# Loading x transposed through ScalarE's queue instead of SyncE's, in a one-core decoder block

## The chip, the core and the metric

One Trainium2 chip, one of its cores. The metric is the device time of one execution in microseconds. Before the change three runs took 345.40, 346.83 and 347.18 us; the median is 346.83.

## What is computed

One layer of a decoder, 256 positions of width 1024, all in float32:

```python
hn = rmsnorm(x, g_attn)
qkv = hn @ w_in                               # 1024 x 3072
ya = rmsnorm(dilated_mixture(qa, ka, va), g_out_a)   # 8 heads
yb = rmsnorm(moba_attention(qb, kb, vb), g_out_b)    # 8 heads
h = x + concat(ya, yb) @ w_out
h = h + square(relu(rmsnorm(h, g_mlp) @ w_up)) @ w_down
gate = sigmoid(rmsnorm(h, g_ple) @ w_ple_gate + b_ple_gate)
h = h + gate * (p @ w_ple_proj)
return rmsnorm(h, g_final)
```

## The kernel before

Every float32 product is made of three matmuls (`mm3`, L149 to L153): each operand is split into a high part that TensorE takes in its fast float32 format and the rest, and high times high, high times low and low times high are summed. So each block of weights, once landed in a `raw` tile, is rounded by ScalarE into `hi` (L75) and the rest is taken by VectorE into `lo` (L76), and the activations are split likewise. The gain of a norm is multiplied into the weights by the same two instructions. The reciprocal root mean square of x is applied after the product: to the values by ScalarE (L419), to q and k by VectorE with a tile `rb` (L299, L300).

The first projection runs by k, the eight slices of 128 of the width: for each k the value weights (`slabs_in[0]`) against x, then the weights of two pairs of heads (`slabs_in[1]`). To let this start early, its loads are cut into small pieces that SyncE's queue issues in the order of use (L203 to L226): `head`, which holds the gains and x for k = 0, then for each k the two weight blocks, and between them `xT` for k = 1, for 2 and 3, and for 4 to 7 (`x_load`, L210). ScalarE's first instructions are a copy that makes it load its table of functions (L202), and then the splits of x and the weights as they land.

While k runs, ScalarE and VectorE sum the squares of x (`x_squares`, L256). At step 33 of the first unit `x_stats` (L274) sums them over the features with two small matmuls (L271), takes mean plus epsilon on VectorE (L183) and its power of -1/2 on GpSimd (L184), and makes a diagonal matrix of it on VectorE (L278). At step 42 `x_bcast` (L282) spreads it over the partitions with two matmuls (L285), and VectorE copies the result to `rb` (L286). At step 46 `make_bias` (L311) has GpSimd make the bias of the first pair of heads out of `consts`: two operations at L316 and two at L318. A bias has two buffers. Scores follow (`scores`, L320): twelve matmuls at L328, evacuated by VectorE with the bias (L334, L337), exponentials on ScalarE (L343), their scaling on GpSimd (L349), transposes on TensorE (`turn`, L359), and the product with the values (L371, L372).

The steps of the units are written in one order. A scheduler of the framework then orders each engine's instructions by its own estimate of when their inputs are there, under the constraint that `issue_after` (L133, L138) sets at the places shown. So an engine's order can move where the source does not. SyncE's and ScalarE's queues share eight semaphore lanes for their transfers: a transfer waits on its queue until the one that had its lane last has landed.

```python
{33: [x_stats], 42: [x_bcast], 46: [VE(0), B_(0, 0)], 48: [E_(0, 0)]}   # L480
```

Of the kernel before, what the change touches and what calls it, by code (L numbers as in the profile page):

```python
# [32 lines left out]
def block_kernel(ctx: ExitStack, tc: tile.TileContext, a: dict):  # L33
    nc = tc.nc
# [135 lines left out]
    stat = outer.tile([P, 64], F32, name="stat")  # L170
    mhalf = outer.tile([P, 2], F32, name="mhalf")
# [23 lines left out]
    xT = ap.tile([P, KT, S], F32, tag="xy", name="xT")  # L195
# [3 lines left out]
    for s in slabs_in[0] + slabs_in[1]:  # L199
        s.raw = wraw.tile([P, 4, 512], F32, tag="raw", name="raw")  # L200
        s.load = lambda: None
    nc.scalar.copy(stat[:, 63:], mhalf[:, :1])  # L202
    nc.sync.dma_start(head, a["head"])  # L203
    halves = [slice(0, 256), slice(256, 512)]

    def block_load(u, k0, k1, col=slice(0, 512)):
        s, r = slabs_in[u][k0 // 4], slice(k0 % 4, (k1 - 1) % 4 + 1)
        nc.sync.dma_start(s.raw[:, r, col], s.src[:, r, col])  # L208

    def x_load(k0, k1):  # L210
        nc.sync.dma_start(xT[:, k0:k1], a["xT"][:, k0:k1])

    for col in halves:
        block_load(0, 0, 1, col)
    block_load(1, 0, 1)
    x_load(1, 2)
    for u in range(2):
        block_load(u, 1, 2)
    x_load(2, 4)
    for k in (2, 3):  # L220
        for u in range(2):
            block_load(u, k, k + 1)
    x_load(4, 8)
    for k in (4, 6):
        for u in range(2):
            block_load(u, k, k + 2)  # L226
# [574 lines left out]
```

## Time and profile before

| What | Value |
|---|---|
| median of three runs | 346.83 us |
| the profiled execution | 347.6 us |
| its span, first to last instruction | 345.8 us |
| mean granted clock of TensorE | 0.982 |
| busy: TensorE, VectorE, ScalarE, GpSimd | 333.2, 216.8, 199.8, 74.1 us |
| DMA, mean over the span | 176 GB/s |

The profile is of one execution, 0.8 us above the median. Busy time alone does not tell where time can be had: the views that do are the waits of each engine, its instructions in order of time, and the chain of waits that ended last. Lines in the rows are those of the kernel before; behind the change all lines from L227 on are smaller by one.

### The profile page before, as it was taken

The numbers are of one execution on the slowest core, as the hardware profiler recorded it, in microseconds if no ns is written. First come the engines' busy times: TensorE is split into PE (matmuls) and PEld (weight loads), VectorE is DVE, ScalarE is ACT, GpSimd is POOL, SyncE is SP. The second block draws the span as 40 slices with busy tenths as digits, with TensorE's granted clock in tenths as the row PEclk, the third lists the DMA queues.
The fourth block names the chain that finished last, engine by engine and source line by source line (L and its number), as shares of the span: only waits on it lengthen the run. The fifth ranks groups of instructions, "written<-read, shape, count | busy, mean of one in ns | idle before, by whom it ended". The sixth has DMA issues, their size and how long they took to land.

```text
span 345.8 us, 5641 instructions
## 1 busy us (share of the span) xinstructions
PE 333.2 (96%) x2188; PEld 298.9 (86%) x2188; DVE 216.8 (63%) x380; ACT 199.8 (58%) x378; POOL 74.1 (21%) x103
## 2 busy tenths in 40 slices
PE   8899899999999999999999999999999999999990
PEld 8699779899877889898998988989989899888890
DVE  4789948687837769537537275292553843758563
ACT  6786838677664668728255374373652825458431
POOL 0025563455214001311020110110201102000443
PEclk9999969999999999999999999999999999999996
DMA  7998951404444369653727618357194463700011
GB/s 193 372 401 289 316 187 53 160 33 159 163 170 159 112 236 321 206 213 115 261 116 248 237 46 320 123 173 263 51 327 159 136 242 110 243 2 1 2 62 61
DMA packets 10971, 60.87 MB, mean 176 GB/s; under 512 B 1216, under 2 KB 1984, under 8 KB 4416
## 3 DMA queue, kind: packets, MB, share of 16 engines
q1 hardware_dynamic: 10944, 60.51, 49.4%
q8 instruction: 17, 0.28, 0.4%
q14 instruction: 10, 0.08, 0.1%
HBM read 59.46 MB, written 1.05 MB: 175 GB/s over the span
## 4 chain that ended last, share of the span: by engine, by line
PE 92%; DMA 2%; POOL 2%; DVE 1%; SPq 1%; ACT 0%; issue 0%; POOLq 0%; DVEq 0%
PE ps L151 29%; PE ps L152 28%; PE ps L153 28%; DMA raw<-in_w_in 2%; PE ps L328 2%; PE ps L371 2%; PE ps L359 2%; PE ps L519 1%; POOL pb L349 1%; SPq L208 1%; PE ps L372 1%; POOL bias L318 1%; DVE lo L76 0%; POOL bias L316 0%; PE ps L271 0%
## 5 line engine op out<-in xcount | busy, mean ns | idle before, releaser
L76 DVE SCALAR_TENSOR_TENSOR lo<-raw,head,hi 128x512 fp32r<-128x512 f32 (+2 forms) x137 | 105.0, 813 | 24.9 <-ACT hi L75 24.6
L75 ACT ACTIVATE hi<-raw,head 128x512 fp32r<-128x512 f32 (+2 forms) x137 | 92.7, 733 | 25.2 <-PE ps L152 11.1
L151 PE MATMUL ps<-hhi,hi 128*128 128x256 f32 x256 | 72.6, 283 | 0.0
L153 PE MATMUL ps<-hhi,lo 128*128 128x256 f32 x256 | 72.5, 283 | 0.0
L152 PE MATMUL ps<-hlo,hi 128*128 128x256 f32 x256 | 72.4, 283 | 0.0
L84 DVE TENSOR_TENSOR lo<-raw,hi 128x1024 fp32r<-128x1024 f32 x34 | 41.5, 1254 | 28.1 <-ACT hi L83 28.0
L583 POOL TENSOR_TENSOR sq<-r 128x512 f32<-128x512 f32 (+1 forms) x18 | 19.9, 1108 | 141.8 <-ACT r L581 141.8
L151 PE MATMUL ps<-hi,u 128*128 128x512 f32 x128 | 50.2, 392 | 0.0
L83 ACT ACTIVATE hi<-raw 128x1024 fp32r<-128x1024 f32 x34 | 34.3, 1052 | 27.2 <-PE ps L153 25.5
L152 PE MATMUL ps<-lo,u 128*128 128x512 f32 x128 | 49.9, 390 | 0.0
L153 PE MATMUL ps<-hi,u 128*128 128x512 f32 x128 | 49.8, 389 | 0.0
L152 PEld LDWEIGHTS ps<-hlo,hi 128*128 128x128 f32 x256 | 49.1, 192 | 0.3
L151 PEld LDWEIGHTS ps<-hhi,hi 128*128 128x128 f32 x256 | 49.1, 192 | 0.3
L153 PEld LDWEIGHTS ps<-hhi,lo 128*128 128x128 f32 x256 | 49.1, 192 | 0.0
L151 PE MATMUL ps<-xhi,hi 128*128 128x256 f32 x128 | 38.7, 303 | 0.0
L152 PE MATMUL ps<-xlo,hi 128*128 128x256 f32 x128 | 36.9, 289 | 0.0
L153 PE MATMUL ps<-xhi,lo 128*128 128x256 f32 x128 | 36.7, 289 | 0.0
L586 DVE TENSOR_TENSOR u<-sq,u 128x512 fp32r<-128x512 f32 (+1 forms) x18 | 11.7, 650 | 34.0 <-ACT u L585 34.0
L153 PEld LDWEIGHTS ps<-hi,u 128*128 128x128 f32 x128 | 24.0, 188 | 5.1
L151 PEld LDWEIGHTS ps<-hi,u 128*128 128x128 f32 x128 | 24.1, 188 | 4.7
L152 PEld LDWEIGHTS ps<-lo,u 128*128 128x128 f32 x128 | 24.1, 188 | 4.7
L151 PEld LDWEIGHTS ps<-xhi,hi 128*128 128x128 f32 x128 | 25.2, 197 | 1.5 <-issue 0.7
(128 smaller groups left out, 531.7 us busy)
## 6 DMA issues: line engine op xcount, KB each, us to landing
raw<-in_w_up SPq DMA_DIRECT2D x16, 1024.0 KB, 5.1
raw<-in_w_down SPq DMA_DIRECT2D x16, 1024.0 KB, 4.8
raw<-in_w_in SPq DMA_DIRECT2D x8, 1024.0 KB, 7.2
raw<-in_w_out SPq DMA_DIRECT2D x4, 1024.0 KB, 4.9
raw<-in_w_gate SPq DMA_DIRECT2D x4, 1024.0 KB, 5.1
raw<-in_w_in SPq DMA_DIRECT2D x4, 512.0 KB, 8.8
raw<-in_w_in SPq DMA_DIRECT2D x7, 256.0 KB, 7.0
h_sb<-in_x SPq DMA_DIRECT2D x1, 1024.0 KB, 7.4
```

Of the source, the lines that this page charges most:

```text
L75: nc.scalar.activation(h, r, AF.Copy, scale=sc)
L76: nc.vector.scalar_tensor_tensor(l, r, sc, h.bitcast(F32), op0=ALU.mult, op1=ALU.subtract)
L83: nc.scalar.activation(h, r, AF.Copy)
L84: nc.vector.tensor_tensor(l, r, h.bitcast(F32), op=ALU.subtract)
L151: nc.tensor.matmul(ps, lhs[0], rhs[0], start=start, stop=False)
L152: nc.tensor.matmul(ps, lhs[0], rhs[1], start=False, stop=False)
L153: last_mm[0] = nc.tensor.matmul(ps, lhs[1], rhs[0], start=False, stop=stop)
L328: last_mm[0] = nc.tensor.matmul(ps[h][:, c : c + w], d["q"][a_][r, q0 : q0 + P], d["k"][b_][r, :w], start=i == 0, stop=i == 2)
L359: nc.tensor.transpose(ps[:, c * P : (c + 1) * P], d["p"][:, h, c * P : (c + 1) * P], ident)
L371: nc.tensor.matmul(o[:, :S], v[:, 0, cols], d["pT"][h][:, :S], start=True, stop=False)
L583: nc.gpsimd.tensor_tensor(sq, r, r, op=ALU.mult)
L586: nc.vector.tensor_tensor(o[1], sq, o[0].bitcast(F32), op=ALU.subtract)
```

## The change

The three transfers of `xT` are issued by ScalarE's queue, ahead of the copy that loads its table. SyncE's queue keeps `head`, the weights and the tables.

```diff
-    nc.scalar.copy(stat[:, 63:], mhalf[:, :1])
     nc.sync.dma_start(head, a["head"])
...
     def x_load(k0, k1):
-        nc.sync.dma_start(xT[:, k0:k1], a["xT"][:, k0:k1])
+        nc.scalar.dma_start(xT[:, k0:k1], a["xT"][:, k0:k1])
+
+
+    x_load(1, 2)
+    x_load(2, 4)
+    x_load(4, 8)
+    nc.scalar.copy(stat[:, 63:], mhalf[:, :1])
     for col in halves:
         block_load(0, 0, 1, col)
     block_load(1, 0, 1)
-    x_load(1, 2)
-    for u in range(2):
-        block_load(u, 1, 2)
-    x_load(2, 4)
-    for k in (2, 3):
+    for k in (1, 2, 3):
         for u in range(2):
             block_load(u, k, k + 1)
-    x_load(4, 8)
     for k in (4, 6):
         for u in range(2):
             block_load(u, k, k + 2)
```

On ScalarE's queue, at the start of the program, the issues stand ahead of the table load (`stat` is the copy's target, `xhi` the high part of x). Before:

```order
L202 ACT_TABLE_LOAD
L202 COPY stat<-mhalf 128x1 [waits DVE_49]
L230 ACTIVATE xhi<-head 128x256 [waits DMAHW0_49]
L261 ACTIVATE xsq<-head 128x256
L75 ACTIVATE hi<-raw,head 128x256 [waits DMAHW1_49]
```

and now:

```order
L210 DMA xT<-in_xT 128x256
L210 DMA xT<-in_xT 128x512
L210 DMA xT<-in_xT 128x1024
L216 ACT_TABLE_LOAD
L216 COPY stat<-mhalf 128x1 [waits DVE_49]
L229 ACTIVATE xhi<-head 128x256 [waits DMAHW1_49]
L75 ACTIVATE hi<-raw,head 128x256 [waits DMAHW3_49]
```

Three issues have come in front, and the square of the first slice has gone behind the first splits of weights.

On GpSimd, behind the constants at the program's start, the scheduler gives another order too. Before, the power of x's mean square (`stat<-stat,mhalf`) is first, and two biases follow, (0, 0) and (0, 1):

```order
L184 ISA
L184 TENSOR_TENSOR stat<-stat,mhalf 128x2 [waits DVE_49]
L316 TENSOR_SCALAR bias<-consts 128x256 [waits DMAHW3_49]
L316 TENSOR_SCALAR bias<-consts 128x256
L318 TENSOR_TENSOR bias<-bias,consts 128x256 [waits Pool_49] x2
L316 TENSOR_SCALAR bias<-consts 128x256 x2
L318 TENSOR_TENSOR bias<-bias,consts 128x256 [waits Pool_49] x2
L316 TENSOR_SCALAR bias<-consts 128x256 [waits DVE_49]
```

and now:

```order
L315 ISA
L315 TENSOR_SCALAR bias<-consts 128x256 [waits DMAHW3_49]
L315 TENSOR_SCALAR bias<-consts 128x256
L317 TENSOR_TENSOR bias<-bias,consts 128x256 [waits Pool_49] x2
L315 TENSOR_SCALAR bias<-consts 128x256 x2
L317 TENSOR_TENSOR bias<-bias,consts 128x256 [waits Pool_49] x2
L184 TENSOR_TENSOR stat<-stat,mhalf 128x2 [waits DVE_49]
L315 TENSOR_SCALAR bias<-consts 128x256 [waits DVE_49]
```

The power has moved behind both biases and so behind the landing of `consts`.

On VectorE, from the mean square of x (L183) to the first evacuations of q and k, before:

```order
L183 TENSOR_SCALAR stat<-ps_339 128x2 [waits PE_49]
L278 TENSOR_SCALAR diag<-ident,stat 128x128 [waits DMAHW1_49,Pool_49]
L278 TENSOR_SCALAR diag<-ident,stat 128x128
L76 SCALAR_TENSOR_TENSOR lo<-raw,head,hi 128x512 [waits DMAHW2_49,Activation_49]
L76 SCALAR_TENSOR_TENSOR lo<-raw,head,hi 128x512 [waits Activation_49] x3
L286 COPY rb<-ps_384 128x256 [waits PE_49]
L299 TENSOR_TENSOR q<-ps_242,rb 128x256 [waits DVE_49,PE_49]
```

and now:

```order
L183 TENSOR_SCALAR stat<-ps_339 128x2 [waits PE_49]
L277 TENSOR_SCALAR diag<-ident,stat 128x128 [waits DMAHW1_49,Pool_49]
L277 TENSOR_SCALAR diag<-ident,stat 128x128
L76 SCALAR_TENSOR_TENSOR lo<-raw,head,hi 128x512 [waits DMAHW2_49,Activation_49]
L76 SCALAR_TENSOR_TENSOR lo<-raw,head,hi 128x512 [waits Activation_49] x3
L76 SCALAR_TENSOR_TENSOR lo<-raw,head,hi 128x512 [waits DMAHW4_49,Activation_49]
L76 SCALAR_TENSOR_TENSOR lo<-raw,head,hi 128x512 [waits Activation_49]
L285 COPY rb<-ps_384 128x256 [waits PE_49]
L76 SCALAR_TENSOR_TENSOR lo<-raw,head,hi 128x512
L298 TENSOR_TENSOR q<-ps_242,rb 128x256 [waits DVE_49,PE_49]
```

Two splits of the next weights have come between the diagonal and `rb`, and one more between `rb` and q. Further on, the four evacuations of the first scores (L334, L337; now L333, L336) stand in one piece, where two splits and a split of k stood among them.

## Rows read from the trace of the kernel before

**Rows 1.** The waits of TensorE (PE) over the whole execution: the waiting line, the one that ended the wait, us in total, how many, the longest in us.

```profile
PE ps L359 <- POOL pb L349: 2.3, 2, 2.0
PE ps L151 <- ACT hi L75: 1.1, 1, 1.1
...
PE ps L152 <- DVE lo L76: 0.3, 1, 0.3
```

**Rows 2.** Busy time by stage: the stretch and its length in us, then busy us and number of instructions of PE, PE's weight loads, VectorE, ScalarE and GpSimd, the granted clock of PE, the busy share of the DMA engines and what they moved in GB/s.

```profile
0.00:50.00 50.00, 45.35 (x312) 41.23 (x314) 38.02 (x83) 34.12 (x73) 17.27 (x29) 0.93 0.86 303
50.00:100.00 50.00, 50.00 (x395) 44.80 (x392) 36.55 (x106) 34.29 (x94) 20.81 (x36) 1.00 0.34 128
```

**Rows 3.** Two pieces of the chain of waits that ended last: start in us, length in us, what it was. The first is the transfer of the value weights for k = 2, the second six transposes of a later pair of heads at full clock.

```profile
4.48 6.98 DMA raw<-in_w_in
...
55.13 0.66 PE ps L359 x6
```

**Rows 4.** TensorE's instructions in order of time: start in us, length in us, engine, line, operation, what it writes from what, tile, how many, and in brackets the idle time in front of it and what ended it.

```profile
12.26 0.50 PE L151 MATMUL ps<-hi,xhi 128*128 128x512 f32 x1 [1.06 <-ACT hi L75]
13.05 0.50 PE L152 MATMUL ps<-lo,xhi 128*128 128x512 f32 x1 [0.28 <-DVE lo L76]
...
27.47 0.61 PE L285 MATMUL ps<-diag,ones 128*128 128x128 f32 x4
...
33.71 0.91 PE L328 MATMUL ps<-k,q 64*128 64x256 f32 x12
...
36.43 0.28 PE L151 MATMUL ps<-xhi,hi 128*128 128x256 f32 x1
...
38.59 0.28 PE L151 MATMUL ps<-xhi,hi 128*128 128x256 f32 x1
...
41.29 0.28 PE L153 MATMUL ps<-xhi,lo 128*128 128x256 f32 x1
43.58 0.90 PE L359 MATMUL ps<-ident,pb 128*128 128x128 f32 x3 [2.01 <-POOL pb L349]
44.81 0.90 PE L359 MATMUL ps<-ident,pb 128*128 128x128 f32 x3 [0.33 <-POOL pb L349]
45.36 0.56 PE L151 MATMUL ps<-xhi,hi 128*128 128x256 f32 x1
...
49.48 0.99 PE L371 MATMUL ps<-pT,vt 128*64 128x256 f32 x4
```

**Rows 5.** One microsecond behind those transposes, columns: length, busy us and instructions of PE, granted clock, DMA share, GB/s.

```profile
47.00:48.00 1.00, 1.00 (x6) 0.50 0.72 164
```

**Rows 6.** The three issues of xT by SyncE's queue: line, queue, operation, shortest, median and longest duration in ns, first and last start.

```profile
L211 SPq DMA_DIRECT2D xT<-in_xT x3: 432/442/1331, 2.6 to 6.4; - x3
```

**Rows 7.** DMA in two microseconds of the start, columns as in rows 5.

```profile
4.00:5.00 1.00, 1.00 (x7) 1.00 0.74 132
...
12.00:13.00 1.00, 0.50 (x1) 1.00 1.05 424
```

**Rows 8.** ScalarE's first instructions in order of time, columns as in rows 4.

```profile
0.72 1.28 ACT L202 ACT_TABLE_LOAD   x1 [0.72 <-PEq L794]
...
2.99 0.42 ACT L230 ACTIVATE xhi<-head 128x256 fp32r<-128x256 f32 x1 [0.79 <-DMA head<-in_head]
```

**Rows 9.** GpSimd's instructions in order of time, columns as in rows 4: the power, the biases of the first two head pairs, and the third bias with the scaling of the first probabilities.

```profile
23.91 0.72 POOL L184 TENSOR_TENSOR stat<-stat,mhalf 128x2 f32<-128x2 f32 x1 [23.49 <-DVE stat L183]
24.72 1.50 POOL L316 TENSOR_SCALAR bias<-consts 128x256 f32<-128x256 f32 x2
...
29.87 1.44 POOL L318 TENSOR_TENSOR bias<-bias,consts 128x256 f32<-128x256 f32 x2
38.70 1.21 POOL L316 TENSOR_SCALAR bias<-consts 128x256 f32<-128x256 f32 x2 [7.39 <-DVE nm L337]
...
41.87 2.89 POOL L349 TENSOR_SCALAR pb<-pb,nm 128x256 f32<-128x256 f32 x4
```

**Rows 10.** The transfer of consts by its line: durations of the issue in ns with first and last start, and us from issue to landing.

```profile
L240 SPq DMA_DIRECT2D consts<-in_consts x1: 432/432/432, 15.1 to 15.1; - x1
...
DMA to landing us min/median/max: 8.8/8.8/8.8
```

**Rows 11.** The two kinds of operation that make a bias, by line: shortest, median and longest duration in ns.

```profile
L316 POOL TENSOR_SCALAR bias<-consts x16: 403/406/931, 24.7 to 79.2; 128x256 f32<-128x256 f32 x16
...
L318 POOL TENSOR_TENSOR bias<-bias,consts x8: 731/738/1184, 26.3 to 47.4; 128x256 f32<-128x256 f32 x8
```

**Rows 12.** VectorE's instructions in order of time, columns as in rows 4: splits of weights (L76), the diagonal, q's and k's splits, the score evacuations of the second pair of heads from the first to the split behind the last.

```profile
17.49 1.41 DVE L76 SCALAR_TENSOR_TENSOR lo<-raw,head,hi 128x512 fp32r<-128x512 f32 x2
...
24.66 0.63 DVE L278 TENSOR_SCALAR diag<-ident,stat 128x128 f32<-128x128 f32 x2 [0.84 <-POOL stat L184]
25.21 3.84 DVE L76 SCALAR_TENSOR_TENSOR lo<-raw,head,hi 128x512 fp32r<-128x512 f32 x4
...
32.44 0.41 DVE L304 TENSOR_TENSOR q<-q 128x256 fp32r<-128x256 f32 x1
32.78 0.41 DVE L306 TENSOR_TENSOR k<-k 128x256 fp32r<-128x256 f32 x1
...
43.99 0.41 DVE L334 CUSTOM_DVE_ANT_0 sc<-ps,bias 128x256 f32<-128x256 f32 x1
...
45.10 0.74 DVE L76 SCALAR_TENSOR_TENSOR lo<-raw,head,hi 128x512 fp32r<-128x512 f32 x1
```

## The prediction

> **What bounds the kernel now.** I read the waits of TensorE first. Over the whole execution it has three that matter, 2.3, 1.1 and 0.3 us [rows 1]; the rows of TensorE below place them all ahead of 45 us. The busy table says the same by stage: TensorE has 45.35 us of work in the first 50 and is busy for all of the next 50 [rows 2]. So the end of the program is the moment at which TensorE comes out of the first 50 us, plus work that never waits; what the change does there goes to the end one for one, and what it does to any other engine counts only where TensorE then waits.
>
> Next the early part. TensorE's wait of 1.1 us ends when the block of value weights for k = 2 has landed and been split; the chain of waits shows this transfer taking 6.98 us from its issue at 4.48 [rows 3]. The last place is the transposes of the first pair of heads (L359): matmuls stop at 41.57 (41.29 plus 0.28), the transposes start at 43.58 and at 44.81, and the matmuls behind them run at 45.36 to 49.48 what the same 18 matmuls did from 36.43 to 38.59 [rows 4]: 4.12 us against 2.16, since the granted clock in that stretch is 0.50, the 1.2 GHz level [rows 5]. Six transposes at full clock take 0.66 us [rows 3], here 1.78. So this place costs 2.01 + 1.12 + 1.96 = 5.1 us.
>
> **The change, part by part.**
>
> SyncE's queue loses three issues, which took 0.43, 0.44 and 1.33 us of it [rows 6]: the weights behind each are issued up to 0.4, 0.9 and 2.2 us sooner. That is cover, not gain: the block that TensorE waited for was issued at 4.48 and spent 6.98 us after that [rows 3], so its bytes, not its issue, were late. I count one effect on the transfers. In the fifth microsecond the engines moved 132 GB/s, against 424 in the thirteenth [rows 7]; with a second queue holding work this dip should mostly close, some 0.2 MB or 0.5 us at the later rate. Bounds: nothing saved, or all 2.2 us of issue.
>
> The Trainium skill speaks against more than that: its page "DMA: Bandwidth & Descriptors", section "Issuing engines are not separate DMA queues", says that starting transfers from several engines saves only the sequencer's time to start them. By that rule the dip would stay too and the sum below would be 0.5 us longer.
>
> ScalarE gets the three issues ahead of its table load. Load and copy run from 0.72 to 2.20 (2.99 less the idle 0.79), and the first activation at 2.99 waits for the transfer of head [rows 8]. No row shows an issue on ScalarE; nearest are SyncE's 0.43 to 1.33 [rows 6]. At 0.44 each they take 1.3, so the first activation comes at 0.72 + 1.3 + 1.5 = 3.5, 0.5 late; the upper bound, 2.2 us in all, makes it 1.4 late. Both are covered by the next term; without that cover they would go to the end.
>
> GpSimd is where the change is largest, though the diff does not touch it. The power that makes x's reciprocal root mean square (L184) stood first and ran at 23.91; behind it came the eight operations that make the biases of two head pairs, to 31.31 [rows 9]. In the changed order the eight come first. They wait for consts, issued at 15.1 and landed 8.8 us later, at 23.9 [rows 10]; the same bytes stand in front of it as before, so I take 23.4 with the 0.5 from above (bounds 21.7 and 24.9, the later one if the transfer ahead of it is issued a microsecond late because its buffer is split later). The eight cost between 4 x 0.406 + 4 x 0.738 = 4.6 us by their medians [rows 11] and 6.6 us as they ran [rows 9]. I take 4.8, the medians and 0.2 for hand-overs, because the slow ones ran beside VectorE's splits of 25.21 to 29.05 [rows 12] and now VectorE will stand at the diagonal, waiting for this very power. That gives 28.2; the power adds 0.72 [rows 9] and a hand-over, 29.0; the diagonal 0.63 [rows 12], 29.7. TensorE's two broadcast matmuls (L285) need it and stand ahead of every later matmul. They ran at 27.47 [rows 4], when the diagonal had been ready since 25.29, a slack of 2.2. Now they run at 29.8: **+2.3 us** (0.4 to 5.6 by the bounds). What is hidden under it: a TensorE that reaches L285 up to 2.3 late.
>
> VectorE's order behind the diagonal changes as well. Six splits instead of four stand ahead of rb. A split takes 0.70, or 0.96 beside GpSimd, q's or k's split about 0.34 [rows 12]. From the diagonal, 6 x 0.70, rb 0.35, a split 0.70, three evacuations of 0.35, a split 0.70 and two of 0.34: 7.7 us until k's lower part is there. TensorE comes to the scores 6.24 us after L285 (33.71 less 27.47) [rows 4]. It can start two of the matmuls without that part: a wait of about **+1.2 us**.
>
> Then the transposes again. Behind k: split, evacuation, two small ones, two splits, 3.2 us, so 10.9 after the diagonal; the four score evacuations, now in one piece, took 1.11 from 43.99 to 45.10 [rows 12], 12.0. GpSimd then makes the third bias and scales: 38.70 to 41.87, and from there 1.71 to the first transpose and 2.94 to the second [rows 4, 9]: 16.9 and 18.1 after the diagonal. TensorE, from its scores at 7.5, needs 7.86 (33.71 to 41.57) [rows 4] and is there at 15.4. It waits 1.5 instead of 2.01. Whether the clock falls decides the rest. It fell after a wait of 2.01 with another 0.9 behind the first three transposes; it did not after 1.06 and 0.28 about 12 us [rows 4, 7]. Now 1.5 and 0.9 are due, 2.4 in all, nearer to the 2.9: I take it that it falls, for 1.5 + 1.12 + 1.96 = 4.6. If it stays, 2.6.
>
> The sum: 2.3 + 1.2 + 4.6 - 5.1 = **+3.0 us**. The profiled execution took 347.6 around its span of 345.8, 0.8 above the median of 346.83; on the median the forecast is 349.8.
>
> **The rivals.**
>
> Even: the same delay, but the clock stays at its upper level at the transposes. 2.3 + 1.2 + 2.6 - 5.1 = +1.0, 347.8. For it: the wait is shorter than the one that dropped the clock. If instead TensorE pays at L285 with a drop, it comes to the scores later, does not wait there, and the transposes find their data: the same end within half a microsecond.
>
> Faster: the transfers gain more than their order says, consts lands so early that the biases are done before the power's input is there, and the weights end TensorE's early waits. TensorE would reach L285 by 26.2 (27.47 less 1.06 and 0.28 [rows 4]), so the power must end by 25.4, the biases by 24.6 and consts land by 19.8, 4.1 us sooner than now. From there the gain is 1.3 plus some 1.5 of the wait at the transposes, 344.0. For it: several seconds of the early table are far below 424 GB/s [rows 7]. Against it: the same 6.5 MB stand in front of consts.
>
> Slower still: x's 896 KB share the engines with the first weights. The blocks for k = 1 and 2 then have up to 512 KB more in front, 1.2 us at 424 GB/s and 4.0 at 132 [rows 7], and ScalarE starts 0.5 to 1.4 late. Below 2.3 all of it is hidden under L285; above, TensorE itself is late. With 3.8 the sum is 1.5 longer: 351.3. For it: in the fifth microsecond the weights had the engines almost alone with 128 KB of x, and were slow already [rows 7].
>
> The Trainium skill, in the same page, section "Queues, rings and completion order", has each engine take turns between the queues that hold work, a packet at a time. By this x and the weights would share from the first packet, which is this rival's mechanism; no row here shows two loaded queues.
>
> **How the numbers follow.** A change within 0.5% (1.7 us) is about what a measurement of this kernel can't tell from none. Chances: forecast 0.40, even 0.30, faster 0.15, slower still 0.15. Of the forecast's 0.40 the bounds of consts and of the biases put about 0.05 within 0.5%; of slower still 0.03 comes out even, because later waits absorb it; of even 0.03 goes over the line. So slower 0.40 - 0.05 + 0.12 + 0.03 = 0.50, same 0.35, faster 0.15. The range runs from 345.0, which leaves out most of the faster case, to 352.3, which holds slower still and the forecast with biases at 6.6; about 2 in 10 is outside. The likeliest case alone spans 347.9 to 352.
>
> **What would show it.** Right: in the changed profile GpSimd's first work is a bias that starts at about 23.4 as consts lands, L184 ends near 29, VectorE idles behind L183 until its diagonal, and TensorE has a wait of 1 to 3 us ahead of L285 (L284 in the new numbering) that ends with the diagonal; then a short wait at the scores, and one of 1 to 2 us at the transposes with the clock at 0.50 behind it. Wrong: consts landed at 20 or before, or TensorE at L285 without a wait, or its longest wait ahead of the value weights of k = 1 or 2 with the clock low there. If the first activation comes later than 4.2, an issue on ScalarE costs more than SyncE's rows say.

## The result

The changed kernel takes 350.29 us (median of 4 runs, 349.11 to 350.89) against 346.53 for the kernel before (4 runs): ratio 1.010, 95% interval 1.007 to 1.013. It is slower, by 3.8 us.

The profiled execution took 349.11 around a span of 347.3, 1.5 more than that of before. Its mean granted clock is 0.995, and its clock did not fall behind the first transposes. The other three runs have no trace, only a mean of 0.977 to 0.982. In the traces of this study, a mean of 0.982 or 0.983 goes with a long stretch at a clock of 0.50 at the transposes (43.4 to 50.2 us in the kernel before; also experiments 3 and 7), 0.990 or 0.991 with a shorter one (47.7 to 51.1 in experiment 1; also 4 and 10, and 2 behind its broadcast), and 0.992 or more with none there (the changed kernel, 5, 6, 8, 9 and 11). The kernel before mixes likewise: of 82 runs beside the experiments, 9 with a mean of 0.994 or more have a median of 345.20, 54 with 0.987 to 0.991 have 346.3, and 19 with less have 347.64. Like with like, the change costs 349.11 - 345.20 = 3.9 us without a fall, by one run, and 350.65 - 347.64 = 3.0 with the long one, if those three fell like that.

**TensorE.** The first fence holds its waits over the whole execution (columns of [rows 1]).

```profile
PE ps L358 <- POOL pb L348: 2.8, 2, 1.7
PE ps L151 <- ACT hi L75: 2.4, 2, 1.4
...
PE ps L151 <- DVE rb L285: 0.6, 1, 0.6
```

The waits at the transposes remain, the two for weights have moved from 12 us to the very start, and there is none at the broadcast L284, where the prediction looked for one of 1 to 3 us. In order of time (columns of [rows 4]):

```profile
5.79 0.80 PE L151 MATMUL ps<-hi,xhi 128*128 128x256 f32 x2 [1.43 <-ACT hi L75]
...
8.48 0.58 PE L151 MATMUL ps<-hi,xhi 128*128 128x256 f32 x1 [0.95 <-ACT hi L75]
...
11.94 0.41 PE L153 MATMUL ps<-xhi,lo 128*128 128x256 f32 x1
12.15 0.41 PE L151 MATMUL ps<-xhi,hi 128*128 128x256 f32 x1
...
12.53 0.28 PE L153 MATMUL ps<-xhi,lo 128*128 128x256 f32 x1
12.64 0.40 PE L151 MATMUL ps<-hi,xhi 128*128 128x512 f32 x1
...
30.14 0.68 PE L284 MATMUL ps<-diag,ones 128*128 128x128 f32 x4
34.56 0.38 PE L151 MATMUL ps<-xhi,hi 128*128 128x256 f32 x1 [0.55 <-DVE rb L285]
...
37.26 1.07 PE L327 MATMUL ps<-k,q 64*128 64x256 f32 x12
...
47.00 0.55 PE L358 MATMUL ps<-ident,pb 128*128 128x128 f32 x3 [1.70 <-POOL pb L348]
48.66 0.55 PE L358 MATMUL ps<-ident,pb 128*128 128x128 f32 x3 [1.11 <-POOL pb L348]
```

The matmuls of k = 1 (the first 128x512 one) start at 12.64; before they started at 7.91. Until 12.4 matmuls of 256 columns follow each other every 0.21 us, from 12.53 every 0.12. Three rows of the kernel before tell what that means: the start of its k = 1, and two like matmuls in the microsecond of [rows 5], 0.22 apart at a granted clock of 0.50:

```profile
7.91 0.63 PE L151 MATMUL ps<-hi,xhi 128*128 128x512 f32 x2
...
47.00 0.41 PE L152 MATMUL ps<-xlo,hi 128*128 128x256 f32 x1
47.22 0.41 PE L153 MATMUL ps<-xhi,lo 128*128 128x256 f32 x1
```

So TensorE ran at the 1.2 GHz level until 12.4, with waits of 1.43 and 0.95 us in that time. At L284 it is 2.67 us later than in [rows 4]: 2.06 of the 4.73 are made up, 1.34 of them because the waits of [rows 4] at 12 and 13 us are gone.

**GpSimd and VectorE** (columns of [rows 9], [rows 12]):

```profile
24.12 0.90 POOL L315 TENSOR_SCALAR bias<-consts 128x256 f32<-128x256 f32 x2 [23.70 <-DMA consts<-in_consts]
...
28.95 0.72 POOL L184 TENSOR_TENSOR stat<-stat,mhalf 128x2 f32<-128x2 f32 x1
42.20 1.64 POOL L315 TENSOR_SCALAR bias<-consts 128x256 f32<-128x256 f32 x2 [12.53 <-DVE nm L336]
...
45.53 3.06 POOL L348 TENSOR_SCALAR pb<-pb,nm 128x256 f32<-128x256 f32 x4
```

```profile
29.71 0.48 DVE L277 TENSOR_SCALAR diag<-ident,stat 128x128 f32<-128x128 f32 x2 [3.35 <-POOL stat L184]
30.11 4.06 DVE L76 SCALAR_TENSOR_TENSOR lo<-raw,head,hi 128x512 fp32r<-128x512 f32 x6
34.09 0.42 DVE L285 COPY rb<-ps 128x256 f32<-128x256 f32 x1
```

The diagonal is being finished as TensorE arrives at L284: two delays end at the same moment, and no wait shows which one counts.

**Queues.** Two issues on SyncE, ScalarE's first instructions (columns of [rows 8]), and two microseconds of DMA (columns of [rows 7]):

```profile
15.77 0.33 SPq L60 DMA_DIRECT2D raw<-in_w_in  x1
16.14 0.43 SPq L239 DMA_DIRECT2D consts<-in_consts  x1
```

```profile
0.72 1.38 ACTq L210 DMA_DIRECT2D xT<-in_xT  x3
...
3.70 0.42 ACT L229 ACTIVATE xhi<-head 128x256 fp32r<-128x256 f32 x1
5.23 0.51 ACT L75 ACTIVATE hi<-raw,head 128x256 fp32r<-128x256 f32 x1 [1.11 <-DMA raw<-in_w_in]
7.92 0.51 ACT L75 ACTIVATE hi<-raw,head 128x256 fp32r<-128x256 f32 x1 [2.18 <-DMA raw<-in_w_in]
```

```profile
4.00:5.00 1.00, 0.36 (x4) 1.00 0.93 290
...
17.00:18.00 1.00, 1.00 (x11) 1.00 0.89 254
```

The fifth microsecond now moves 290 GB/s where [rows 7] have 132, but what it moves is x: ScalarE waits 1.11 and 2.18 us for the two halves of the first value weights. Consts is issued at 16.14, a microsecond later than in [rows 10]: the transfer ahead of it is issued at 15.77, since its buffer waits for a split that VectorE now starts at 14.99, and at 17 us the DMA engines are down to 254 GB/s. Before, that transfer was issued at 14.68:

```profile
14.68 0.33 SPq L60 DMA_DIRECT2D raw<-in_w_in  x1
```

### The profile page after: what moved, and what is told of

Read it like the earlier page. It is cut to its first block, busy times and chain, and to the rows that moved or that the text cites. A ratio compares the mean times of both kernels' runs of the same rounds, so it can differ in the third digit from the quotient of the medians.

```text
span 347.3 us, 5638 instructions
## 1 busy us (share of the span) xinstructions
PE 332.7 (96%) x2188; PEld 298.3 (86%) x2188; DVE 215.1 (62%) x380; ACT 200.0 (58%) x378; POOL 72.2 (21%) x103
## 4 chain that ended last, share of the span: by engine, by line
PE 84%; DMA 4%; DVE 4%; POOL 3%; ACT 2%; issue 1%; SPq 0%; POOLq 0%; DVEq 0%
PE ps L151 26%; PE ps L153 26%; PE ps L152 26%; DMA consts<-in_consts 2%; DMA raw<-in_w_in 2%; DVE lo L76 2%; PE ps L370 2%; PE ps L358 1%; PE ps L327 1%; ACT hi L75 1%; POOL bias L317 1%; PE ps L518 1%; POOL bias L315 1%; POOL pb L348 1%; PE ps L371 1%
## 5 line engine op out<-in xcount | busy, mean ns | idle before, releaser
L76 DVE SCALAR_TENSOR_TENSOR lo<-raw,head,hi 128x512 fp32r<-128x512 f32 (+2 forms) x137 | 103.8, 803 | 26.3 <-ACT hi L75 26.1
L151 PE MATMUL ps<-hi,u 128*128 128x512 f32 x128 | 50.2, 392 | 0.0
```

What stands on the lines that cost most here:

```text
L76: nc.vector.scalar_tensor_tensor(l, r, sc, h.bitcast(F32), op0=ALU.mult, op1=ALU.subtract)
L151: nc.tensor.matmul(ps, lhs[0], rhs[0], start=start, stop=False)
```

## The experiments

The two delays are told apart by undoing each alone (1, 3, 7), by making one of them alone in the kernel before (2), and by mending them in pairs (4, 10, 12). Experiments 5, 6, 8, 9, 11 and 12 take away the waits at the transposes, whose clock blurs the rest. Each ratio is to the kernel before on the same chip, and each time the median of 6 to 12 runs. The last two columns say when the broadcast and the first matmul of k = 1 start in the one profiled execution. The same loads give k = 1 at 7.85 to 9.03 (the kernel before, 5, 2) and, with all of x on ScalarE at once, at 11.43 to 12.64, so differences under 1 us there say little.

| | us | ratio, 95% | L284 at | k = 1 at |
|---|---|---|---|---|
| 1 change, power first | 350.34 | 1.0106 (1.0075 to 1.0137) | 30.23 | 12.24 |
| 2 before, biases first | 349.43 | 1.0092 (1.0059 to 1.0124) | 30.07 | 9.03 |
| 3 512 KB of x on SyncE | 347.15 | 1.0017 (0.9995 to 1.0040) | 27.89 | 10.54 |
| 4 as 1, 80 warm-ups | 348.78 | 1.0058 (1.0033 to 1.0083) | 28.93 | 11.57 |
| 5 before, scalings first | 344.14 | 0.9918 (0.9890 to 0.9946) | 27.51 | 7.85 |
| 6 change, scalings first | 348.03 | 1.0034 (1.0015 to 1.0053) | 29.79 | 11.85 |
| 7 512 KB issued later | 347.98 | 1.0032 (1.0008 to 1.0056) | 27.71 | 10.35 |
| 8 as 3, scalings first | 344.72 | 0.9937 (0.9913 to 0.9961) | 26.87 | 9.51 |
| 9 as 8, 60 warm-ups | 344.65 | 0.9944 (0.9925 to 0.9962) | 27.38 | 10.02 |
| 10 change, 80 warm-ups | 350.61 | 1.0115 (1.0087 to 1.0143) | 29.80 | 11.64 |
| 11 as 4, scalings first | 346.21 | 1.0001 (0.9981 to 1.0021) | 28.79 | 11.43 |
| 12 as 6, power first | 347.91 | 1.0050 (1.0029 to 1.0071) | 29.17 | 11.81 |

**1. The change, power first.** `make_bias` for the first two pairs is issued after the power; no other engine's order differs.

```
...
     B_ = lambda g, j: (lambda: make_bias(g, j))   # becomes, for (g, j) < (0, 2):
+        with tc.issue_after(pw[0].ins):            # pw[0]: the power of L184
+            make_bias(g, j)
```

> The changed kernel with one thing undone: on GpSimd the power (L184) stands ahead of the eight bias operations again; every other engine keeps its order. Theory A (the delay of the broadcast L284 from 27.5 to 30.1 us is GpSimd's order): the power ends by 27.1, and L284 runs at 27.5 to 28; the time comes back to 346.5 to 347. Theory B (TensorE itself comes late, since x took the engines from the first weights and the clock was at its lower level until 12.4): L284 stays at 30.0, and what goes is only what follows it on VectorE: the 0.55 us wait at rb and 1 to 2 us of the waits at the transposes, so 348 to 348.5.

Theory B in its place, L284 at 30.23, but not in its time: 348 to 348.5 was expected, and the time is the change's. Three pieces of this kernel's trace, GpSimd, TensorE and a microsecond behind the transposes:

```profile
26.68 0.72 POOL L184 TENSOR_TENSOR stat<-stat,mhalf 128x2 f32<-128x2 f32 x1 [26.25 <-DVE stat L183]
```

```profile
30.23 0.61 PE L284 MATMUL ps<-diag,ones 128*128 128x128 f32 x4
...
36.51 1.22 PE L327 MATMUL ps<-k,q 64*128 64x256 f32 x12
```

```profile
48.00:49.00 1.00, 0.96 (x5) 0.50 0.69 106
```

The power runs 2.3 us sooner, and TensorE is where it was. The scores start 0.75 sooner, 6.28 behind L284 instead of 7.12, so the six splits ahead of rb do their harm only when the diagonal is late too; in this execution the fallen clock at the transposes (0.50) took that back. The waits there, 1.69 and 1.11 us, did not shrink as expected.

**2. The kernel before, biases first.** `B_(0, 0)` and `B_(0, 1)` are moved in front of `x_stats`, and the power issued after them; TensorE's order is held up to the scores, and on VectorE the four splits ahead of rb remain.

```
...
-             {33: [x_stats], 42: [x_bcast], 46: [VE(0), B_(0, 0)], 48: [E_(0, 0)]}, 60, 33),
+             {33: [B_(0, 0), B_(0, 1), x_stats], 42: [x_bcast], 46: [VE(0)], 48: [E_(0, 0)]}, 60, 33),
```

> The kernel before, x still on SyncE's queue, with the one thing done to it that the change did on GpSimd: the eight bias operations stand ahead of the power, and the order of TensorE is as before. Theory A: L285 moves from 27.5 to 29.8 or 30, and the time is 349 to 350.5, all of the loss. Theory B alone (GpSimd's order is covered) would leave it at 346.5 to 347.

Theory A, as expected, with the wait in the open (L293 is the broadcast here):

```profile
30.07 0.94 PE L293 MATMUL ps<-diag,ones 128*128 128x128 f32 x4 [1.80 <-DVE diag L286]
```

Behind that wait the clock fell as well, and the scores come 7.86 us behind the broadcast instead of 6.24:

```profile
31.00:32.00 1.00, 1.00 (x4) 0.50 0.04 16
```

So GpSimd's order alone costs 0.9%, in a run that pays for a fallen clock too; all the rest of the change, x's transfers and the new orders of VectorE and ScalarE, costs 1.1% alone (1); together they cost 1.0%. They lie side by side.

**3. The 512 KB of x back on SyncE,** at its old place; the two small transfers stay on ScalarE (`x_load` takes the queue as a third argument).

```
...
     x_load(2, 4)
-    x_load(4, 8)
     nc.scalar.copy(stat[:, 63:], mhalf[:, :1])
...
+    x_load(4, 8, nc.sync)
     for k in (4, 6):
```

> The changed kernel, but the largest of the three transfers of x (k = 4 to 7, 512 KB) is issued by SyncE where it was before; the two small ones stay on ScalarE. GpSimd has the power first again by itself. Theory B (those 512 KB starve the first weights): the value weights of k = 0 land at 4 to 5.5 instead of 7.9, the matmuls of k = 1 start at 8 to 9.5 instead of 12.6, L284 runs at 27 to 28 and the time is 345 to 347. If not the large transfer but the second queue as such, or ScalarE's later start, makes TensorE late: k = 1 still starts after 11, and the time is 348 or more.

L284 and the time come back to within 0.4 and 0.8 us of the kernel before. The middle of the expectation was missed: k = 1 starts at 10.54. Even with 384 KB on a second queue the first weights come later (the first real matmul runs at 5.49 after a wait of 1.14, against 4.17 with none before), and matmuls of 256 columns came every 0.21 us until 10.0; in experiment 8, with the same loads, they came every 0.12 from 6.8 on, and k = 1 started at 9.51.

**7. The 512 KB issued later,** by ScalarE, behind x's split for k = 1; power first.

```
-    x_load(4, 8)
...
+            if k == 1:
+                x_load(4, 8)
             qk[k]()
```

> All three transfers of x on ScalarE's queue as in the change, but the 512 KB one is issued only after x's split for k = 1, and GpSimd has the power ahead of the biases. If those 512 KB ahead of the first weights are the cause of TensorE's lateness: the matmuls of k = 1 start at 9 to 10.5 instead of 12.6, L284 runs at 27 to 28, and the time is 346 to 347. If the second queue itself is the cause, L284 stays at 29.5 or later and the time at 349 or more.

k = 1 and L284 as expected, so it is the 512 KB in front and not the second queue as such; the time is 1 us above. TensorE's waits at the transposes are 2.02 and 0.76 here, and seven of twelve runs have a mean clock of 0.982, with 347.73 to 348.91; the other five lie at 346.22 to 347.55.

**4 and 10. 80 warm-up matmuls,** with the power first (4) and without (10). Warm-ups are matmuls on a constant tile at the start of the program; the 30 of the kernel run from 0.97 to 4.35 us.

```
-WARM = 30
+WARM = 80
```

> The first kernel (power ahead of the biases) with 80 warm-up matmuls instead of 30 ahead of the program, which end after 5.5 and bridge most of TensorE's wait for the first weights. If the low clock from 5.8 to 12.4 is the larger part of TensorE's lateness: the granted clock is 1.0 from about 6 on, k = 1 starts at 10.2 to 10.8 (when its weights have landed and been split) instead of 12.6, L284 at 27.7 to 28.3, and the time is about 2 us below the first kernel's. If landing alone makes it late, k = 1 still starts at 12 or later, or waits return there, and the time is the first kernel's within 0.5.

> The changed kernel with 80 warm-up matmuls and nothing else: TensorE no longer late by its clock, the power still behind the eight biases. If the two delays lie side by side, TensorE now reaches L284 at 28.5 to 29 and waits there about 1 us for the diagonal, L284 stays at 29.8 to 30.2 and the time at 349.5 to 350.5. If GpSimd's order costs nothing in the changed kernel, L284 runs at 28.9 and the time is 348.8, as with the power first.

In 4 the 256-column matmuls run every 0.12 us from 7.8 on. TensorE gains 1.3 us at L284, less than expected: the last warm-ups run until 7.76, past the first weights (ScalarE splits them at 4.89), and the second half of the value weights is split only at 7.80. In 10 the same gain is lost to the diagonal:

```profile
29.80 0.68 PE L284 MATMUL ps<-diag,ones 128*128 128x128 f32 x4 [0.64 <-DVE diag L277]
```

Against the change's 350.29, either mend alone gives nothing (350.34, 350.61), both give 1.5 us (348.78).

**5 and 6. Scalings first,** in the kernel before and in the changed one: the bias two pairs on is issued after the scalings of a pair.

```
     def B_(g, j): ...
+        if (g, j) >= (0, 2):
+            es.enter_context(tc.issue_after(pbi[divmod(4 * g + j - 2, 4)].ins))
```

> The kernel before, with one thing moved on GpSimd: the four scalings of a pair's probabilities stand ahead of the bias two pairs later, so that the first transposes wait for the reciprocal (39.90) and not for the third bias (38.70 to 41.87). Theory: the first scaling starts at 40.1 instead of 41.87, the first transposes at 41.8 instead of 43.58, the second at 43.0 to 43.5; the clock stays at 1.00 there, so the term that the prediction priced at 5.1 us falls to 1 or 1.5, and the time to 342.5 to 343.5. Rival: the bias that now comes later is the next wait, at the scores or the transposes of the second or third pair, and the time gains under 1.5.

> The changed kernel with the same thing moved on GpSimd, the scalings ahead of the bias two pairs later; the power still stands behind the eight bias operations. The first scaling starts at 43.7 instead of 45.53, TensorE waits 0.1 instead of 1.70 at the first transposes and up to 1 at the second, and the clock does not fall; L284 stays at 30. The time is 346.5 to 347.5, and against the same edit of the kernel before the change costs 3.5 to 5: all of the early delay, with the transposes no longer giving any of it back.

In 5, TensorE's rows at the place of [rows 4] and GpSimd's scalings:

```profile
41.63 0.55 PE L359 MATMUL ps<-ident,pb 128*128 128x128 f32 x3
...
43.02 0.55 PE L359 MATMUL ps<-ident,pb 128*128 128x128 f32 x3 [0.85 <-POOL pb L349]
...
46.16 0.66 PE L371 MATMUL ps<-pT,vt 128*64 128x256 f32 x4 [0.44 <-DVE pT L361]
```

```profile
40.06 2.90 POOL L349 TENSOR_SCALAR pb<-pb,nm 128x256 f32<-128x256 f32 x4 [8.69 <-DVE nm L345]
```

The first wait is gone, the clock stays, and the value matmuls come 3.3 us sooner than in [rows 4]; all six runs have a mean clock of 0.992 or more. At 344.14 this is the lowest median of the study, though expected at 342.5 to 343.5. Experiment 6 costs 3.9 us more, as expected (3.5 to 5), though its time is above the 346.5 to 347.5: with nothing at the transposes to blur it, the change costs 3.9. Of the 3.5 between the two profiled executions 2.3 is there at L284, 2.8 at the scores and 3.5 at the third pair's scores; what is added last is the subject of experiment 11.

**12. Power and scalings first,** the change otherwise.

> The sixth kernel (the change, scalings ahead of the later bias) with the power ahead of the eight biases as well, and 30 warm-up matmuls. It prices GpSimd's order of the power in the changed kernel where no clock falls at the transposes: L284 stays at 29.8 to 30.2 (TensorE's own lateness), the scores start 6.3 behind it instead of 6.8 to 7.1, so the time is 0.3 to 0.8 below the sixth kernel's 348.03: 347.2 to 347.7. If the order were a cause of its own here, it would be 346 or less.

347.91 is experiment 6 within 0.1, a little above what was expected: the power's place is worth nothing in the changed kernel while TensorE is late. The profiled execution, with L284 at 29.17, is the fastest of the nine runs (347.03).

**11, 8 and 9.** The edits of 4 and 5 together; of 3 and 5; and the latter with `WARM = 60`.

> The change as it stands on the queues (all of x on ScalarE, at once) with everything else mended: power first, 80 warm-up matmuls, scalings ahead of the later bias. L284 at 28.9 as in the fourth kernel, no wait of over 1 us at the transposes, the clock at 1.00; 345.5 to 346.5. What is left against the same scalings in the kernel before, 1.5 to 2.5 us, is then the price of the 512 KB ahead of the first weights.

> The third kernel (512 KB of x back on SyncE, the two small transfers on ScalarE, power first by itself) with the scalings ahead of the bias two pairs later. With the waits at the transposes gone it shows what the two small transfers on a second queue are worth: L284 at 27.9 against 27.5 in the kernel before says 0.4 us slower than the same edit of the kernel before, 343 to 344; if the small transfers gain something that the transposes hid, it is below that one.

> The eighth kernel (512 KB of x on SyncE, two small transfers on ScalarE, power first, scalings ahead of the later bias) with 60 warm-up matmuls instead of 30, which bridge TensorE's 1.7 us wait for the first weights: the clock should be at its upper level from 6 on, k = 1 start at 8.5 to 9 instead of 9.5, L284 run 0.7 to 1.2 sooner, and the time be 343.2 to 344.2, below every kernel so far. If the transfers end TensorE's waits instead, a wait ahead of k = 1 or 2 returns and the time is the eighth kernel's.

In 11 the change has cost 346.21 - 344.14 = 2.1 us against experiment 5, within the 1.5 to 2.5 expected. Not all of it is the price of x's bytes: L284 is 1.28 us later than in 5 (28.79 against 27.51), and 0.8 us more are lost behind the transposes. From the second transposes to the third pair's scores 11 takes 7.45 us (44.30 to 51.75) and 5 takes 6.64 (43.02 to 49.66), because the scheduler gave VectorE and ScalarE another order there: ScalarE copies its half of the transposed probabilities (`pT`) at 47.73, 3.43 behind the second transposes, in 5 at 45.65, 2.63 behind. The products with the values, one group in 5, fall in two:

```profile
47.22 0.65 PE L370 MATMUL ps<-pT,vt 128*64 128x256 f32 x2 [0.23 <-DVE pT L360]
...
48.25 0.65 PE L370 MATMUL ps<-pT,vt 128*64 128x256 f32 x2 [0.16 <-ACT pT L360]
```

Between 11 and 12 only the warm-ups differ, so the 1.7 us between their medians are what the low clock and the gaps of the start cost; the two profiled executions are only 0.4 apart, at L284 and in the time, since that of 12 had its clock up early. Experiment 8 is not faster than 5, although its profiled execution has L284 0.6 sooner: two small transfers on a second queue gain nothing in the medians. Experiment 9 missed: the real matmuls start only at 7.07, behind the warm-ups, against 6.04 in 8, and the orders of VectorE, ScalarE and GpSimd shifted with it, so no gain is shown and the warm-ups' own worth stays open there.

## Why the prediction was right

The time (349.8 forecast, 350.29 measured) and the place of the loss were right; the cause was half of it. Of the signs that the prediction named, those on GpSimd and VectorE came, but the wait ahead of L284 did not, and "TensorE at L285 without a wait" was its own sign of being wrong.

- **GpSimd's order**, +2.3: as written. Consts lets the biases start at 24.12, 0.7 later than taken, they take 4.83 us to the power (4.8 forecast), the diagonal is there at 30.2 (29.7) and L284 runs at 30.14 (29.8). Experiment 2 shows the step by itself: 2.6 us at the broadcast. In the changed kernel it is hidden, since TensorE is as late.
- **The cover** was the step that failed. The prediction put "a TensorE that reaches L285 up to 2.3 late" under this term and gave lateness beyond that to a rival of 0.15. TensorE was 2.7 late of its own (experiment 1), which is the rival's mechanism with 2.7 in place of 3.8. The sum needs only the larger of two delays, and they were equal by chance; so the number held by luck, and "undo the order" as a cure would have given nothing.
- **Its size** had a part that no term held: the clock. The prediction read the clock at the transposes and not at the start, where TensorE stayed at the 1.2 GHz level until 12.4 (until about 5.8 before). With the gap bridged by warm-ups, L284 comes 1.3 us sooner (4 against 1), and the time is 1.7 lower (11 against 12). How long the low stretch lasts differs between executions: in 1 it lasts until 13.5, in 8 it is over by 6.8 in spite of a wait of 1.69, and in 12 the clock was up, then fell to 0.50 from 8.1 to 11.6. What decides it is not shown.
- **The transfers**, -0.5: did not come. The dip closed (290 against 132 GB/s), but consts landed no sooner, because the transfer ahead of it waited for its buffer, the upper bound named. The Trainium skill's rule (page "DMA: Bandwidth & Descriptors", section "Issuing engines are not separate DMA queues") that only the sequencer's time is saved would have left the sum 0.5 higher, which is nearer; but the trace shows more than saved issue time, since the rate did rise. The Trainium skill's rule of taking turns between queues (same page, section "Queues, rings and completion order") fits: ScalarE got the first half of the value weights at 5.2 and the second at 7.9, while x's 896 KB moved (before, both from 3.6 on).
- **ScalarE**: 3.5 forecast, 3.70 measured; three issues in 1.38 us (1.3 forecast), and covered, as said.
- **The scores**, +1.2: 37.26 is 0.88 later behind L284 than in [rows 4], of which 0.55 is a wait at rb and not at k. Experiment 1 removes it with the late diagonal.
- **The transposes**: waits of 1.70 and 1.11 where 1.5 and 0.9 were forecast; the 0.9 that the prediction read in [rows 4] is the length of the first transposes, the idle time behind them is 0.33. Whether the clock then falls differs from run to run. The profiled execution is the even rival's case: +1.0 forecast for it, +1.5 measured against the profiled one of before. The fall was priced at 1.96 us and part of the 1.12; the outer groups of runs of before are 347.64 - 345.20 = 2.4 apart, and experiment 5 shows that this place was there to be mended all along.

## What to carry to other kernels

Moving a transfer to an idle queue does not move only its issue: its bytes come forward too, and the work that is needed first must still be first, over all queues together. Where two engines become late at one join, undo both before you judge either: each one alone hides the other. And look at the clock wherever an engine starts with gaps, not only where the profile's clock column shows a fall.

## What was not expected of the hardware

- From 4 to 8 us, while x came by a second queue, the DMA engines moved 290 to 363 GB/s; before, with one queue, 132 to 335. In the two microseconds after x had landed, one queue alone moved 381 and 399 (219 and 219 before), so the second queue by itself is not shown to be the reason.
- The clock column says 1.00 in every microsecond ahead of 12 us in the changed kernel, while matmuls of 256 columns follow each other every 0.21 us and, later, every 0.12. The trace's record of the granted clock begins only where that spacing changes (12.44 us here, 5.82 before), and ahead of it the column shows 1.00. At the start, the spacing of like matmuls is what tells the level, and the mean clock of a run leaves that stretch out.
- The same waits end with a fallen clock in one execution and not in another: the clock of experiment 1 fell after waits of 1.69 and 1.11 us at the transposes, that of the changed kernel's profiled execution did not after 1.70 and 1.11. The kernel before fell after 2.01 in its profiled execution, and the groups of its runs with the highest and the lowest mean clock are 2.4 us apart in the median.
